# Attention steps that are due within two groups of matmuls, taken ahead of a product's evictions and of weight splits

## The chip, the cores and the metric

The kernel runs on one core of one Trainium2 chip. The metric is device time in microseconds (us), lower is better. Before the change three timed runs gave 1688.29, 1689.68 and 1690.58, a median of 1689.68.

## What is computed

One layer of a decoder trunk in float32, over 2048 tokens of width 1024. `u` is the modulated input; one wide product makes queries, keys, values and gates; a sliding-window attention (16 query heads, 2 key heads, window 128, a learned bias and one "sink" logit per head) and a multi-scale causal pool run side by side; two projections, a gated sum, an output projection and a layer norm follow.

```python
u = x * (1.0 + scale[:, None, :]) + shift[:, None, :]
h = u @ w_in[l]
q, k, v, a_gate, p_in, p_gate, m_a, m_p = jnp.split(h, offsets, axis=-1)
a = sliding_window_sink_attention(q, k, v, sinks[l], bias, mask) * jax.nn.silu(a_gate)
a = a @ w_attn_proj[l]
p = jnp.einsum('bsgc,gcd->bsgd', multiscale_causal_pool(p_in), w_pool_mix[l]).reshape(B, S, POOL_WIDTH)
p = ((p * pool_scale[l]) * jax.nn.silu(p_gate)) @ w_pool_proj[l]
y = jax.nn.sigmoid(m_a) * a + jax.nn.sigmoid(m_p) * p
y = (y @ w_out[l]) * (1.0 + gate[:, None, :])
x = layer_norm(DEEPNORM_ALPHA * x + y, ln_gain[l], ln_bias[l])
```

## The kernel before

**Products.** A float32 operand is split into two halves (`hi`, a rounded copy, and `lo`, the rest), and one matmul becomes three: hi by hi, hi by lo, lo by hi (`mm3`). A "group" is such a trio of 128x128 by 128x512 matmuls, and a "product" is four groups, one after the other, into one PSUM bank (`product`, L295). Two neighbouring output tiles by two halves of the tokens are computed with seven products in place of eight, in Strassen's manner. The class `Quad` holds such a four. Its products are called, in order, B11, T1 (stage F), T2, B21 (stage S), T3, B22 (stage Th) and T4 (stage L). A quad that runs alone keeps T4 for later, when it stands between B11 and T1 of the next quad. The moving operands are the tiles `set_B...` and `set_T...`; in the excerpts below T1, T2, T3 and T4 read set_T_67, set_T_159, set_T_411 and set_T_613, and B11, B21 and B22 read set_B_66, set_B_68 and set_B_459.

**Evictions** (`behind`, L460). After each product comes its follow-up. After B11 ACT copies bank a to a third bank c (`mm<-mm`); after T1 ACT copies bank b to a tile p (`p<-mm`); after T2 DVE writes b = c + p (`mm<-mm,p`), which reads the bank c that T3 accumulates into next, so T3 must wait for it; after T3 DVE writes p = c + p (`p<-mm,p`). Four tiles leave through `consume`, after B21, T3, B22 and T4: one ACT instruction, and for queries and two of the gates one DVE instruction that waits for it (`q_hi` then `q_lo`, or `sig` then `sig`). For the pooled input (`px`) and two other gates ACT alone does it.

**Weight splits** (`split_part`, L431). Weights of a stage are split two or three products ahead: ACT casts them (`CAST w_set<-W`), then DVE (for stage Th of a quad that runs alone, POOL) subtracts to get `lo`. A table made by `plan` says at which product each part stands (`before`); `run` (L488) issues the parts ahead of that product's matmuls.

**Attention steps** (`overlay`, L812). In two phases of the program, one for each half of the tokens, 13 quads run alone, 91 products, and attention is woven in: 64 steps and three more to drain the pipeline. Step n (L922) issues on PE the scores of block n (`lg<-kk,qs`), the transposes of block n-2 (`pt<-ident,L`) and the value matmuls of block n-3 (`pv<-...`). On ACT it issues the scaling of block n-1 (`L<-L` with 192 columns, twice), the cast `pth<-pt`, a copy `o<-pv` and the exponentials of block n (`L<-L` with 193 columns, twice). On DVE it issues a reciprocal, two bias-and-minimum instructions (shown as ISA), the subtraction `ptl<-pt,pth` and two additions `st<-pv,o`. POOL writes a small mark, SP loads the next queries. The scores bank `lg` and the transposes bank `pt` exist once: a step's transposes wait until DVE has done `ptl` of the step ahead.

**When a step comes** (`beat`, L978). `product` calls `beat` after each group. Each call adds `rate` to a credit, and at 1 a step is issued there and then; the first 12 calls of a phase, and some in its middle, are rests. With N = 64 and 364 groups, rate is 67 / 316 = 0.212, so that a step comes every 4.7 groups, at any of the four places of a product. All engines take their instructions in the order in which the program issues them, which the kernel keeps by hand (`Ordered`, L50).

Of the kernel before, what the change touches and what calls it, by code (L numbers as in the profile page):

```python
# [59 lines left out]
def kernel(  # L60
# [81 lines left out]
    def cols(t, n):  # L142
        return t[:, n * CH : (n + 1) * CH]
# [13 lines left out]
    def mm3(acc, whi, wlo, uhi, ulo, start, stop, **kw):  # L157
        mm(acc, whi, uhi, start=start, stop=False, **kw)
        mm(acc, whi, ulo, start=False, stop=False, **kw)
        mm(acc, wlo, uhi, start=False, stop=stop, **kw)  # L160

    def bank(tag="mm"):
        if tag in ("c1", "pv"):
            return phase_ps["now"].tile([P, CH], F32, tag=tag, bufs=phase_ps["pv"] if tag == "pv" else 1, name=tag)
        return ps.tile([P, CH], F32, tag=tag, bufs=4 if tag == "mm" else 1, name=tag)
# [129 lines left out]
    def product(acc, w, name, first=False, i0=0, i1=4, beat=None):  # L295
        t = sets[name]
        hi, lo = w
        for i in range(i0, i1):
            cols = slice(i * P, (i + 1) * P)
            mm3(  # L300
                acc,
                hi[:, cols],
                lo[:, cols],
                t[:, i, 0, :],
                t[:, i, 1, :],
                first and i == 0,
                i == 3,
                skip_group_check=True,
            )
            if beat:  # L310
                beat()
# [3 lines left out]
    def defer(ticks, f, local=False):  # L315
        due.append((now[0] + ticks, len(due), f, local))

    def run_due(every=False, local=False):
        while due and (every or any(d[0] <= now[0] or local and d[3] for d in due)):
            d = min((d for d in due if every or d[0] <= now[0] or local and d[3]), key=lambda d: d[:2])  # L320
            due.remove(d)
            d[2]()

    def at(p, f):
        assert p >= now[0], (p, now[0])
        hooks.setdefault(int(p), []).append(f)
# [5 lines left out]
    def tick():  # L332
        for f in hooks.pop(now[0], ()):
            f()
        now[0] += 1
        run_due()
# [89 lines left out]
    def split_part(ph, q, kind, part):  # L426
        if part == 0 and kind in q.parts:
            q.made = kind
        if kind == getattr(q, "made", None):
            return  # L430
        raw = {"F": q.first, "S": q.second, "Th": q.third, "L": lambda: q.a22}[kind]()  # L431
        if kind == "L":
            if part == 0:
                t = q.parts["L"] = ph.split(*q.rings[kind])
                act.copy(t[:, 0:CH], raw)
            else:
                t = q.parts["L"]
                low(dve, t[:, CH:], raw, t[:, 0:CH])
            return
        if part == 0:  # L440
            hi, lo = q.parts[kind] = [ph.split(x) for x in q.rings[kind]]
            act.copy(by_two(hi), raw)
            return
        hi, lo = q.parts[kind]
        low(pool if kind == "Th" and not q.pair and not q.tail else dve, by_two(lo), raw, by_two(hi))
        if kind == "F":
            q.mid(pool)
            defer(2, lambda q=q: q.keep_sum(1))
        if kind == "S":
            q.late(pool)  # L450

    def weights_of(q, kind, h):
        if kind == "L":
            t = q.parts["L"]
            return t[:, 0:CH], t[:, CH:]
        hi, lo = q.parts[kind]
        return cols(hi, h), cols(lo, h)

    def behind(ph, q, kind, h):
        if kind == "F":  # L460
            if h == 0:
                q.c = bank(("lg", "c1")[q.x] if q.pair else "mm")
                if q.pair and q.x in ph.fresh:
                    t = sets["B11"][:, 0, 0, :]
                    mm(q.c, t[:, 0:P], t, start=True, stop=True, skip_group_check=True)
                    ph.fresh.remove(q.x)
                act.copy(q.c, q.a)
            else:
                q.p5 = ph.p("p5")
                act.copy(q.p5, q.b)  # L470
        elif kind == "S":
            if h == 0:
                if not q.summed:
                    dve.tensor_tensor(q.b, q.c, q.p5, ALU.add)
            else:
                q.consume(ph, 0, 0, q.a)
        elif kind == "Th":
            if h == 0:
                dve.tensor_tensor(q.p5, q.c, q.p5, ALU.add)
                q.consume(ph, 1, 1, q.p5)  # L480
            else:
                q.consume(ph, 0, 1, q.b)
        else:
            q.consume(ph, 1, 0, q.c)
# [3 lines left out]
    def run(phases, products, before, loads):  # L488
        starts = {z["first"]: z for z in phases}
        ph, leave, beat = None, None, None  # L490
        for p, (q, kind, h, name) in enumerate(products):
            if p in starts:
                phase = starts[p]
                if phase["pools"] is not ph:
                    if ph:
                        if leave:
                            leave()
                        run_due(True)
                        ph.__exit__(None, None, None)
                    ph = phase["pools"].__enter__()  # L500
                leave, beat = None, None
                more = phase["enter"](ph, phase)
                if more:
                    beat, leave = more
            assert now[0] == p
            done = q.opened and kind in "FS"
            for z, k, part in before.get(p, ()):
                if not (z.opened and k in "FS"):
                    split_part(ph, z, k, part)
            for z, what in loads.get(p, ()):  # L510
                if what == "w":
                    z.load_w(ph)
                elif what == "last":
                    z.load_last(ph, z.own)
                elif what == "sum":
                    if not z.again:
                        z.sum1()
                        defer(1, lambda z=z: z.keep_sum(0))
                else:
                    z.prefetch(ph, *what)  # L520
            if done:
                if kind == "S" and h:
                    at(p + LATER[q.x, "S"], lambda q=q: behind(ph, q, "S", 1))
                if kind == "F":
                    now[0] += 1
                    continue
            else:
                if kind == "F" and h == 0:
                    q.a, q.b = bank(), bank()
                acc = {"B11": "a", "T1": "b", "T2": "c", "B21": "a", "T3": "c", "B22": "b", "T4": "c"}[name]  # L530
                product(getattr(q, acc), weights_of(q, kind, h), name, kind == "F", beat=beat)
                for f in mids.pop(p, ()):
                    f()
                if q.opened and kind == "L" and q.x:
                    at(p + LATER[q.x, kind], lambda q=q: behind(ph, q, "L", 0))
                elif q.opened and (q.x, kind) in LATER and not h:
                    at(p + 1, lambda q=q: dve.tensor_tensor(q.p5, q.c, q.p5, ALU.add))
                    at(p + LATER[q.x, kind], lambda q=q: q.consume(ph, 1, 1, q.p5))
                else:
                    behind(ph, q, kind, h)  # L540
            tick()
        run_due(True)
        ph.__exit__(None, None, None)
# [247 lines left out]
    def overlay(ph, s, n_slots):  # L791
# [3 lines left out]
        N = KT * U  # L795
# [179 lines left out]
        state = [0, 0.0, 12]  # L975
        rate = (N + 3) / (n_slots - 48.0)

        def beat():  # L978
            n, credit, rest = state
            if rest:  # L980
                state[2] -= 1
                return
            state[1] += rate
            if state[1] >= 1 and n < N + 3:
                step(n)
                state[0] += 1
                state[1] -= 1
                if n == N // 2 - 1:
                    load_k(1)
                    state[2] = 8  # L990
                if n == N // 2 + 2:
                    load_v(1)
                    state[2] = 5
# [689 lines left out]
    for i, (groups, store) in enumerate(parts):  # L1683
        phase(mix_pools, groups, out_part(i, store))
    run(phases, *plan(phases))


# [51 lines left out]
```

## Time and profile before

| | us |
|---|---|
| median of three runs | 1689.68 |
| the profiled execution, its own time | 1685.7 |
| the profiled execution, first to last instruction (span) | 1683.8 |
| first attention phase, the stretch 150 to 470 | 320 |
| second attention phase, the stretch 728 to 1046 | 318 |

The page's first part gives each engine's busy time: PE 98%, DVE 69%, ACT 57%, POOL 35%. PE's granted clock is 90% or more in all of the forty slices of its second part but the second one, and 0.994 in the mean over the span. In a row of the timeline stand the start, the duration, the engine, the instruction with what it writes and reads, and in brackets how long the engine sat idle before and what ended that. Matmuls are pipelined: a row's duration overlaps the next row's start, so the distance between starts is what a matmul costs.

### The profile page before, as it was taken

To read this page: it belongs to the slowest core of one execution; us is meant where nothing else is said; L and a number is where in the kernel's file an instruction comes from. 1 tells how busy PE (TensorE), PEld (TensorE's weight loads), DVE (VectorE), ACT (ScalarE), POOL (GpSimd) and SP (SyncE) were. 2 spreads that over 40 slices of the span, in tenths; PEclk is the share of its full clock that TensorE was granted. 3 is DMA by queue.
4 is the path that set the end of the run, shared out by engine and by line. 5 is a ranking of instruction groups with operands and counts; after the bars stand their busy time and mean duration, and the time that the engine had idled before them with its cause. 6 is when DMAs were issued, how large, how long until landed. Compare 5 with 4: busy or idle time off the path is not lost. (4 is left out here: it accounts for less than half of the span.)

```text
span 1683.8 us, 24835 instructions
## 1 busy us (share of the span) xinstructions
PE 1654.8 (98%) x8146; PEld 1392.7 (83%) x8146; DVE 1164.9 (69%) x2161; ACT 962.7 (57%) x1944; POOL 588.4 (35%) x569
## 2 busy tenths in 40 slices
PE   8999999999999999999999999999999999999997
PEld 8888888888888888888888888888888888888885
DVE  6765666665648779546666666587867785878878
ACT  4555878788743346467877777344544343435453
POOL 3112454645552323323334244222332211114544
PEclk9899999999999999999999999999999999999999
DMA  9499777986557799875566553688968686777443
GB/s 349 137 306 302 197 233 203 265 219 202 173 181 234 267 316 309 274 188 163 172 179 202 151 171 127 222 281 304 347 207 303 230 309 203 264 259 266 151 151 124
DMA packets 340896, 384.77 MB, mean 229 GB/s; under 512 B 152200, under 2 KB 203424, under 8 KB 340640
## 3 DMA queue, kind: packets, MB, share of 16 engines
q1 hardware_dynamic: 334880, 376.99, 69.8%
q10 hardware_dynamic: 5856, 6.18, 1.1%
q8 instruction: 64, 1.05, 0.3%
q14 instruction: 64, 0.52, 0.1%
q0 software_dynamic: 32, 0.02, 0.0%
HBM read 238.91 MB, written 145.78 MB: 228 GB/s over the span
## 5 line engine op out<-in xcount | busy, mean ns | idle before, releaser
L56 PE MATMUL mm<-set_B,w_set 128*128 128x512 f32 x2664 | 651.5, 391 | 0.7 <-DVE w_set L56 0.7
L56 PEld LDWEIGHTS mm<-set_B,w_set 128*128 128x128 f32 x2664 | 496.1, 188 | 103.5 <-DVE w_set L56 1.5
L56 POOL TENSOR_TENSOR W<-W 128x512 f32<-128x512 f32 x185 | 268.0, 1459 | 584.2 <-DVE w_set L56 344.9
L56 PE MATMUL mm<-set_T,w_set 128*128 128x512 f32 x1896 | 463.7, 391 | 1.0 <-POOL w_set L56 0.7
L56 PEld LDWEIGHTS mm<-set_T,w_set 128*128 128x128 f32 x1896 | 349.7, 188 | 73.1 <-POOL w_set L56 1.9
L56 DVE TENSOR_TENSOR w_set<-W,w_set 128x1024 fp32r<-128x1024 f32 x197 | 255.5, 1297 | 107.6 <-ACT w_set L56 93.0
L56 ACT CAST w_set<-W 128x1024 fp32r<-128x1024 f32 x222 | 232.2, 1047 | 95.5 <-PE mm L56 55.6
L56 ACT ACTIVATE L<-L 128x193 f32<-128x193 f32 (+5 forms) x512 | 214.9, 446 | 99.5 <-DVE L L56 98.4
L56 PE MATMUL lg<-set_T,w_set 128*128 128x512 f32 x828 | 201.4, 391 | 1.4 <-DVE w_set L56 1.0
L56 PE MATMUL c<-set_T,w_set 128*128 128x512 f32 x828 | 200.8, 390 | 0.0
L56 PEld LDWEIGHTS lg<-set_T,w_set 128*128 128x128 f32 x828 | 155.1, 188 | 34.9 <-DVE w_set L56 1.8
L56 PEld LDWEIGHTS c<-set_T,w_set 128*128 128x128 f32 x828 | 155.5, 188 | 33.0 <-DVE w_set L56 0.8
L56 DVE TENSOR_TENSOR ptl<-pt,pth 128x512 fp32r<-128x512 f32 (+1 forms) x128 | 86.4, 675 | 117.5 <-ACT pth L56 117.5
L56 POOL TENSOR_TENSOR W<-W,A 128x512 f32<-128x512 f32 x41 | 58.1, 1418 | 271.1 <-DMA A<-in_win_dram 106.6
L56 DVE CUSTOM_DVE_ANT_0 L<-lg,bt,nsink 128x192 f32<-128x192 f32 (+2 forms) x256 | 93.6, 404 | 22.3 <-PE lg L56 21.7
L56 ACT ACTIVATE sig<-mm 128x512 f32<-128x512 f32 x76 | 45.5, 599 | 92.8 <-PE mm L56 89.8
L56 PEld LDWEIGHTS lg<-kk,qs 128*128 128x128 f32 x512 | 76.2, 190 | 15.7 <-issue 4.2
L56 POOL TENSOR_TENSOR w_set<-W,w_set 128x1024 fp32r<-128x1024 f32 x25 | 60.9, 2435 | 77.8 <-ACT w_set L56 69.4
L56 PE MATMUL pt<-ident,L 128*128 128x128 f32 x496 | 76.5, 275 | 5.7 <-DVE ptl L56 5.4
L56 PE MATMUL lg<-kk,qs 128*128 128x192 f32 (+2 forms) x512 | 75.8, 270 | 3.6 <-DMA qs<-q_d 2.9
L56 POOL TENSOR_TENSOR st<-st,ag 128x512 f32<-128x512 f32 x32 | 46.5, 1452 | 84.3 <-DVE st L56 78.5
L56 ACT CAST pth<-pt 128x512 fp32r<-128x512 f32 (+1 forms) x128 | 71.9, 562 | 6.4 <-PE pv L56 5.6
(211 smaller groups left out, 1905.9 us busy)
## 6 DMA issues: line engine op xcount, KB each, us to landing
W<-in_win_dram SPq DMA_DIRECT2D x40, 512.0 KB, 5.8
qs<-q_d SPq DMA_DIRECT2D x128, 128.0 KB, 4.3
sums_d<-W SPq DMA_DIRECT2D x62, 256.0 KB, 3.6
W<-sums_d SPq DMA_DIRECT2D x31, 512.0 KB, 3.6
ain_d<-st SPq DMA_DIRECT2D x56, 256.0 KB, 3.6
A<-in_win_dram SPq DMA_DIRECT2D x42, 256.0 KB, 5.5
q_d<-q_hi SPq DMA_DIRECT2D x32, 256.0 KB, 4.1
q_d<-q_lo SPq DMA_DIRECT2D x32, 256.0 KB, 3.9
```

What stands on the lines that cost most here:

```text
L56: return lambda *args, **kw: self.tc.keep_in_program_order(op(*args, **kw))
```

## The change

`beat` gets an argument. With `early=2.0` it adds nothing to the credit, does nothing during a rest, and issues a step when the credit would reach 1 within two more groups. `run` makes such a call at two places: ahead of the weight splits that stand before a product, and after a product's four groups, ahead of its evictions. Right after a product the credit has not changed by the time of the next product's splits, so there the first call finds what the second one left.

```diff
--- before.py
+++ after.py
@@ -504,6 +504,8 @@
                     beat, leave = more
             assert now[0] == p
             done = q.opened and kind in "FS"
+            if beat and p in before:
+                beat(2.0)
             for z, k, part in before.get(p, ()):
                 if not (z.opened and k in "FS"):
                     split_part(ph, z, k, part)
@@ -529,6 +531,8 @@
                     q.a, q.b = bank(), bank()
                 acc = {"B11": "a", "T1": "b", "T2": "c", "B21": "a", "T3": "c", "B22": "b", "T4": "c"}[name]
                 product(getattr(q, acc), weights_of(q, kind, h), name, kind == "F", beat=beat)
+                if beat:
+                    beat(2.0)
                 for f in mids.pop(p, ()):
                     f()
                 if q.opened and kind == "L" and q.x:
@@ -975,13 +979,16 @@
         state = [0, 0.0, 12]
         rate = (N + 3) / (n_slots - 48.0)
 
-        def beat():
+        def beat(early=0.0):
             n, credit, rest = state
+            if rest and early:
+                return
             if rest:
                 state[2] -= 1
                 return
-            state[1] += rate
-            if state[1] >= 1 and n < N + 3:
+            if not early:
+                state[1] += rate
+            if state[1] + early * rate >= 1 and n < N + 3:
                 step(n)
                 state[0] += 1
                 state[1] -= 1
```

A step that fell behind the first or second group of a product (34 of the 67 in each phase) now stands at the end of the product ahead; one that fell behind the third or fourth group stays. By the credit's arithmetic, 46 of the distances between steps were five groups and 18 were four; now 42 are four, 11 five and 11 seven, beside two longer ones at the pauses in each order.

The first place is the start of the first attention phase, on PE: B21 and T3 of the first quad, and the scores of the first two steps. Set names as above. Before:

```order
L56 MATMUL mm<-set_T_159,w_set 128x512 x12
L56 MATMUL mm<-set_B_68,w_set 128x512 x12
L56 MATMUL mm<-set_T_411,w_set 128x512 x3
L56 MATMUL lg<-kk,qs 128x64 x2
L56 MATMUL lg<-kk,qs 128x128 x2
L56 MATMUL mm<-set_T_411,w_set 128x512 x9
L56 MATMUL mm<-set_B_459,w_set 128x512 x6
L56 MATMUL lg<-kk,qs 128x192 x4
L56 MATMUL mm<-set_B_459,w_set 128x512 x6
```

Now:

```order
L56 MATMUL mm<-set_T_159,w_set 128x512 x12
L56 MATMUL mm<-set_B_68,w_set 128x512 x12
L56 MATMUL lg<-kk,qs 128x64 x2
L56 MATMUL lg<-kk,qs 128x128 x2
L56 MATMUL mm<-set_T_411,w_set 128x512 x12
L56 MATMUL lg<-kk,qs 128x192 x4
L56 MATMUL mm<-set_B_459,w_set 128x512 x12
```

The first step's scores moved from behind T3's first group to the end of B21, and the second step's from the middle of B22 to the end of T3.

The second place is in the second phase, where a gate's quad (`sig`) follows a query's quad (`q_hi`); on ACT, from the copy after B11 to the second step behind it. `pth` marks a step; `q_hi<-mm` is the eviction after T4, `p_...<-mm` the one after T1, and `w_set<-W` the cast for stage Th. Before:

```order
L56 COPY mm<-mm 128x512
L56 ACTIVATE q_hi<-mm 128x512
L56 ACTIVATE L<-L 128x192 x2
L56 CAST pth<-pt 128x512
L56 COPY o_8985<-pv 64x256
L56 ACTIVATE L<-L 128x193 x2
L56 COPY p_9005<-mm 128x512
L56 CAST w_set<-W 128x1024
L56 ACTIVATE L<-L 128x192 x2
L56 CAST pth<-pt 128x512
L56 COPY o_9038<-pv 64x256
```

Now:

```order
L56 COPY mm<-mm 128x512
L56 ACTIVATE L<-L 128x192 x2
L56 CAST pth<-pt 128x512
L56 COPY o_8978<-pv 64x256
L56 ACTIVATE L<-L 128x193 x2
L56 ACTIVATE q_hi<-mm 128x512
L56 ACTIVATE L<-L 128x192 x2
L56 CAST pth<-pt 128x512
L56 COPY o_9026<-pv 64x256
L56 ACTIVATE L<-L 128x193 x2
L56 COPY p_9041<-mm 128x512
L56 CAST w_set<-W 128x1024
```

The first of the two steps moved ahead of T4's eviction, the second ahead of T1's eviction and the cast. A little later in the same quad, DVE around the eviction after T2, `mm<-mm,p`. Before:

```order
L56 TENSOR_TENSOR ptl<-pt,pth 128x512
L56 TENSOR_TENSOR st<-pv,o_9038 64x128 x2
L56 TENSOR_TENSOR mm<-mm,p_9005 128x512
L56 RECIPROCAL L<-L 128x2
L56 ISA L<-lg,bt,nsink 128x192
L56 ISA L 128x1
L56 ISA L<-lg,bt,nsink 128x192
L56 ISA L 128x1
L56 TENSOR_TENSOR ptl<-pt,pth 128x512
```

Now:

```order
L56 TENSOR_TENSOR st<-pv,o_9026 64x128 x2
L56 RECIPROCAL L<-L 128x2
L56 ISA L<-lg,bt,nsink 128x192
L56 ISA L 128x1
L56 ISA L<-lg,bt,nsink 128x192
L56 ISA L 128x1
L56 TENSOR_TENSOR ptl<-pt,pth 128x512
L56 TENSOR_TENSOR st<-pv,o_9083 64x128 x2
L56 TENSOR_TENSOR mm<-mm,p_9041 128x512
```

A whole step, with its subtraction `ptl`, moved ahead of the addition after T2.

The third place is two quads earlier, a quad of pooled input, on DVE: splits of stage F and L (`w_set`) and a step. Before:

```order
L56 TENSOR_TENSOR st<-pv,o_8414 64x128 x2
L56 TENSOR_TENSOR w_set<-W,w_set 128x1024
L56 TENSOR_TENSOR w_set<-A_7825,w_set 128x512
L56 RECIPROCAL L<-L 128x2
L56 ISA L<-lg,bt,nsink 128x192
L56 ISA L 128x1
L56 ISA L<-lg,bt,nsink 128x192
L56 ISA L 128x1
L56 TENSOR_TENSOR ptl<-pt,pth 128x512
```

Now:

```order
L56 RECIPROCAL L<-L 128x2
L56 ISA L<-lg,bt,nsink 128x192
L56 ISA L 128x1
L56 ISA L<-lg,bt,nsink 128x192
L56 ISA L 128x1
L56 TENSOR_TENSOR ptl<-pt,pth 128x512
L56 TENSOR_TENSOR st<-pv,o_8454 64x128 x2
L56 TENSOR_TENSOR w_set<-W,w_set 128x1024
L56 TENSOR_TENSOR w_set<-A_7860,w_set 128x512
L56 TENSOR_TENSOR p_8363<-mm,p_8363 128x512
```

The two splits moved from ahead of a step to behind it, and stand right ahead of the addition after T3.

## The prediction

> **What bounds the kernel.** I read the page first, then the stretches of the two attention phases, since the change touches nothing outside them, then PE's waits there.
>
> ```profile
> span 1683.8 us, 24835 instructions
> PE 1654.8 (98%) x8146; PEld 1392.7 (83%) x8146; DVE 1164.9 (69%) x2161; ACT 962.7 (57%) x1944; POOL 588.4 (35%) x569
> ...
> 150.00:470.00 320.00, 314.44 (x1733) 269.07 (x1732) 198.56 (x599) 250.54 (x644) 161.14 (x182) 1.00 0.76 217
> ...
> 728.00:1046.00 318.00, 313.98 (x1755) 270.76 (x1754) 203.15 (x597) 244.31 (x629) 109.78 (x126) 1.00 0.60 169
> ```
>
> PE is busy 98% of the span, and in both phases all but 5.6 and 4.0 us. ACT is busy 250.54 of 320 us (78%) and 244.31 of 318 (77%), DVE 62 and 64%. So PE is the bound, and the order of ACT's and DVE's work matters only where PE waits for it:
>
> ```profile
> PE pt L56 <- DVE ptl L56: 3.4, 9, 0.7
> PE lg L56 <- DMA qs<-q_d: 1.3, 1, 1.3
> ...
> PE pt L56 <- DVE ptl L56: 2.0, 5, 0.7
> PE lg L56 <- DMA qs<-q_d: 1.6, 1, 1.6
> ```
>
> The first two rows are the first phase, the others the second. The transposes wait for the subtraction `ptl` of the step ahead, 3.4 + 2.0 us in 14 places, and the first scores of a phase for a DMA. That is all the change can win: 5.4 us as idle time, perhaps 9 with the slower starts around it. It removes and adds no instruction; it only moves steps.
>
> **How a step hangs together.** A stretch of the second phase on PE, where a gate's quad follows a query's (steps 25 to 29):
>
> ```profile
> 847.12 3.58 PE L56 MATMUL mm<-set_B,w_set 128*128 128x512 f32 x15
> 850.54 0.59 PE L56 MATMUL lg<-kk,qs 128*128 128x192 f32 x4
> 850.96 0.61 PE L56 MATMUL pt<-ident,L 128*128 128x128 f32 x4
> ...
> 855.32 0.59 PE L56 MATMUL lg<-kk,qs 128*128 128x192 f32 x4
> 856.00 0.65 PE L56 MATMUL pt<-ident,L 128*128 128x128 f32 x4
> ...
> 856.97 2.92 PE L56 MATMUL mm<-set_T,w_set 128*128 128x512 f32 x12
> 859.73 0.59 PE L56 MATMUL lg<-kk,qs 128*128 128x192 f32 x4
> 860.56 0.66 PE L56 MATMUL pt<-ident,L 128*128 128x128 f32 x4 [0.25 <-DVE ptl L56]
> ...
> 867.73 2.24 PE L56 MATMUL mm<-set_T,w_set 128*128 128x512 f32 x9
> ```
>
> Fifteen matmuls take 850.54 - 847.12 = 3.42 us, so 0.23 each, 0.69 a group, 2.75 a product. Undisturbed transposes start 0.42 after the scores (850.96 - 850.54), and a step takes about 1.4 us of PE (0.42, and 0.97 from its transposes to the next matmuls, 856.00 to 856.97). Two steps four groups apart start 4.1 us apart, five groups 4.8.
>
> ```profile
> 843.18 0.16 DVE L56 RECIPROCAL L<-L 128x2 f32<-128x2 f32 x1
> 843.43 0.81 ACT L56 ACTIVATE L<-L 128x192 f32<-128x192 f32 x2 [2.12 <-DVE L L56]
> 844.14 0.56 ACT L56 CAST pth<-pt 128x512 fp32r<-128x512 f32 x1
> 844.74 0.69 DVE L56 TENSOR_TENSOR ptl<-pt,pth 128x512 fp32r<-128x512 f32 x1 [0.74 <-ACT pth L56]
> 845.35 0.57 DVE L56 TENSOR_TENSOR st<-pv,o 64x128 f32<-64x128 f32 x2
> 845.80 0.19 ACT L56 ACTIVATION_READ_ACCUMULATOR L<-L 128x1 f32 x1
> 846.67 0.63 ACT L56 ACTIVATE q_hi<-p 128x512 fp32r<-128x512 f32 x1 [0.68 <-DVE p L56]
> 847.34 0.69 DVE L56 SCALAR_TENSOR_TENSOR q_lo<-p,q_hi 128x512 fp32r<-128x512 f32 x1 [0.70 <-ACT q_hi L56]
> ```
>
> This is one step's chain: reciprocal to scaling 0.25, to `pth` 0.71, to `ptl` 0.60, to its end 0.69; `st` ends 2.74 after the reciprocal, the exponentials 1.85 after `pth`. It zigzags between ACT and DVE, and an eviction ahead of it adds its own zigzag (0.63 + 0.69): in the second row ACT sat idle 2.12 us until DVE came to the step. The next step's reciprocal waits for the exponentials of this one. So the chain is nearly serial, and a step moved ahead of evictions gets a short chain, while what it passed gets a long one.
>
> **The change, place by place.**
>
> *Starts of the phases.*
>
> ```profile
> 156.88 0.86 PE L56 MATMUL mm<-set_T,w_set 128*128 128x512 f32 x3
> 159.07 0.63 PE L56 MATMUL lg<-kk,qs 128*128 128x64 f32 x4 [1.34 <-DMA qs<-q_d]
> ...
> 732.13 0.66 PE L56 MATMUL lg<-kk,qs 128*128 128x192 f32 x4 [1.61 <-DMA qs<-q_d]
> ```
>
> The first scores wait for their queries, which are issued at the phase's start, as before. Now they stand ahead of the three matmuls (in both phases) that covered 0.69 us of that wait. **+0.7 twice, +1.4.** Nothing hides this.
>
> *The stretch above: a step behind B11, T4, T1 and T2 each, and T4 of the quad ahead leaves through ACT and DVE* (steps 26 to 29, and 47 to 50 in the same pattern; two places in each phase).
>
> ```profile
> 855.26 0.69 DVE L56 TENSOR_TENSOR ptl<-pt,pth 128x512 fp32r<-128x512 f32 x1 [0.73 <-ACT pth L56]
> 856.53 0.57 ACT L56 COPY mm<-mm 128x512 f32<-128x512 f32 x1
> 861.09 0.59 ACT L56 COPY p<-mm 128x512 f32<-128x512 f32 x1
> 861.58 1.05 ACT L56 CAST w_set<-W 128x1024 fp32r<-128x1024 f32 x1
> 862.52 0.81 ACT L56 ACTIVATE L<-L 128x192 f32<-128x192 f32 x2
> 864.93 0.68 DVE L56 TENSOR_TENSOR mm<-mm,p 128x512 f32<-128x512 f32 x1
> ```
>
> Step 26 does not move; its `ptl` ends at 855.95, so step 27's transposes start at 856.00, as before, but the group that PE did ahead of them is now behind: 0.69 lost. Step 27's chain no longer has T4's eviction ahead: copy at 856.53, scaling 857.1, `pth` 857.8, `ptl` done 859.1, exponentials 859.65. So step 28, at 859.73, starts its transposes at 860.15 and not at 860.56: 0.41 won, 0.28 behind. Then T4's eviction (0.63 + 0.69 with its hand-over) puts step 28's reciprocal at 861.0; scaling 861.25, `pth` 861.95, exponentials done 863.8. Now the copy to p and the cast come (861.09 to 862.52 in the rows, 1.43): step 29's scaling 865.25, `pth` 865.95, `ptl` 866.55, `st` done 867.75, and only then the addition `mm<-mm,p`, done 868.45. PE: step 28 ends 861.1, T2 863.9, step 29 865.25, B21 868.0. T3 writes the bank that this addition reads, so it starts at 868.5; before, with the same steps done, it started at 867.73 (the last PE row), for the addition had gone at 864.93. **+0.75 four times, +3.0.**
>
> The other T2 ends that got a step (seven a phase) have one at B21's end too, so T3 comes 1.4 later (5.5 us after T2's end) and a chain of 2.74 + 0.69 with a cast ahead (1.43) fits. I cost them nothing; if that slack is gone each costs up to 0.75.
>
> *The last two gates' quads* (steps 53 to 55 and 59 to 61).
>
> ```profile
> 1017.38 0.69 PE L56 MATMUL lg<-kk,qs 128*128 128x192 f32 x4
> 1018.81 0.66 PE L56 MATMUL pt<-ident,L 128*128 128x128 f32 x4 [0.74 <-DVE ptl L56]
> ```
>
> Step 60 already waits (1.43 after its scores, not 0.42) and moves one group ahead: 0.69 lost in each phase, as the `ptl` it waits for does not move. At step 54 most of the group is covered; about 0.25 lost. **+1.8 in all.**
>
> *Splits that now follow a step in a pooled quad* (the third place of the change).
>
> ```profile
> 841.45 1.21 DVE L56 TENSOR_TENSOR w_set<-W,w_set 128x1024 fp32r<-128x1024 f32 x1
> 842.58 0.68 DVE L56 TENSOR_TENSOR w_set<-A,w_set 128x512 fp32r<-128x512 f32 x1
> ...
> 813.78 1.72 DVE L56 TENSOR_TENSOR w_set<-A,w_set 128x512 fp32r<-128x512 f32 x1 [0.24 <-ACT w_set L56]
> ```
>
> DVE used to do them while it waited for step 18; now step 18 is awaited first, and 1.9 us of splits (1.21 + 0.68) stand ahead of steps 19 and 20 and so of step 21's transposes. Between nothing (a slack of about one group swallows it) and +1.0 in each phase: I take half, **+1.0 in all**. The same form of split took 0.68 and 1.72 us; the longer one ran beside POOL work. "GPSIMD Engine Reference" of the Trainium skill, section 1, says that GpSimd's SBUF interfaces are shared with VectorE, with contention for DVE instructions that have two SBUF inputs; the two rows agree. By that rule the splits, now beside POOL's five gate operations, cost their long form, and the sum would take the upper end, 1.0 more.
>
> *Won.*
>
> ```profile
> 772.62 0.66 PE L56 MATMUL pt<-ident,L 128*128 128x128 f32 x4 [0.38 <-DVE ptl L56]
> ```
>
> Step 9 waits behind a pile of evictions, with PE idle 0.38. Step 7, moved to T3's end, lets that pile be done earlier: at best **-0.35 twice, -0.7**. Evictions and splits otherwise have two or three products of slack (5 to 8 us) and take the delay of one chain.
>
> **The sum:** 1.4 + 3.0 + 1.8 + 1.0 - 0.7 = +6.5 us. The profiled execution took 1685.7 (span 1683.8), so it would become 1692.2; the three timed runs lie higher, with a median of 1689.68, and against that I predict **1696.2**.
>
> **Rivals.**
> - *Faster.* Moved steps have the short chain, so all waits for `ptl` vanish (5.4 us idle) and T3 never waits: -5.4 + 1.4 = -4.0, 1685.7. For it: the waits named are exactly of this kind, and ACT idles ahead of scalings. It decides if the steps behind B11, which don't move, end `ptl` within 4.5 us of their scores; the stretch above shows 855.95 - 850.54 = 5.4. Chance 0.12.
> - *An exchange.* Waits are won and lost alike, and only the starts and a little remain: +1 to +3, about 1692. For it: delays in a chain that PE leads are partly made up later. Chance 0.26.
> - *Much slower.* T3 waits at all T2 ends with a step, 14 more by 0.5: +7 on the sum, 1703. The weights of T3 may be late as well, since their cast now waits behind a step. Chance 0.15.
> - *It doesn't do what it says.* The call ahead of the splits indeed never issues a step that the call behind a product didn't; but the order of instructions shows half the steps moved, so this rival is out.
>
> My forecast, a loss of 4 to 10 us, has 0.47. About 0.2% (3.4 us) is what a measurement of this kernel can tell from no change. Slower by more than that: 0.47 + 0.15 = 0.62; within: 0.26; faster: 0.12. The range reaches from the faster rival, 1686, to the much slower one, 1704.
>
> **What would show it.** Right: PE's wait for the queries grows from 1.3 and 1.6 to 2.0 and 2.3; waits of PE for `ptl` stay at 5 us or more, at the steps behind T4; a new wait of PE for DVE's `mm<-mm,p`, some 2 us in four places. Wrong: no such new wait, or the waits for `ptl` gone; or T3 waiting for POOL's `w_set`.

## The result and the profile after

The changed kernel took 1695.69 us (median of six runs, 1693.9 to 1697.66) beside 1689.71 for the kernel before (six runs, 1686.37 to 1690.58). The ratio is 1.0038, with a 95% interval of 1.0025 to 1.0051: 6.4 us slower, between 4.2 and 8.6. The profiled execution took 1693.9 us. Two single executions of the kernels reported below ran at a mean granted clock of 0.565 and 0.555 (2718 us in `not_t4`, 2763 us in the kernel before) and are left out of all medians and ratios.

The page of the kernel after, its first part (busy time, share of the span, instructions), then PE's waits in the first attention phase (150 to 475 us) and in the second (728 to 1055 us): total idle us, times, longest.

```profile
span 1692.0 us, 24814 instructions
PE 1655.8 (98%) x8146; PEld 1391.7 (82%) x8146; DVE 1168.5 (69%) x2161; ACT 961.2 (57%) x1944; POOL 592.2 (35%) x569
...
PE pt L56 <- DVE ptl L56: 4.7, 9, 0.8
PE lg L56 <- DMA qs<-q_d: 1.8, 1, 1.8
PE mm L56 <- DVE mm L56: 1.4, 2, 0.7
PE lg L56 <- DVE L L56: 0.9, 3, 0.4
...
PE pt L56 <- DVE ptl L56: 3.2, 6, 0.7
PE lg L56 <- DMA qs<-q_d: 1.4, 1, 1.4
PE lg L56 <- DVE L L56: 0.7, 2, 0.5
PE mm L56 <- DVE mm L56: 0.4, 2, 0.2
```

The work is the same: 8146 matmuls, and PE busy for 1655.8 us against 1654.8. What grew is idle time inside the phases. The waits for `ptl` went from 3.4 + 2.0 to 4.7 + 3.2 us, and a row that did not exist stands at 1.4 + 0.4: PE waits for DVE's `mm<-mm,p`, the addition that T3 has to wait for, in four places. The scores' waits for DVE grew to 0.9 + 0.7; in the kernel before there was this row in the first phase and none in the second:

```profile
PE lg L56 <- DVE L L56: 0.7, 2, 0.5
```

One of those places, in the second phase: PE and DVE of the kernel after, steps 27 to 29 and T3.

```profile
859.40 0.59 PE L56 MATMUL lg<-kk,qs 128*128 128x192 f32 x4
860.50 0.66 PE L56 MATMUL pt<-ident,L 128*128 128x128 f32 x4 [0.51 <-DVE ptl L56]
...
864.22 0.59 PE L56 MATMUL lg<-kk,qs 128*128 128x192 f32 x4
864.65 0.60 PE L56 MATMUL pt<-ident,L 128*128 128x128 f32 x4
...
868.34 0.59 PE L56 MATMUL lg<-kk,qs 128*128 128x192 f32 x4
868.76 0.60 PE L56 MATMUL pt<-ident,L 128*128 128x128 f32 x4
869.67 2.94 PE L56 MATMUL mm<-set_B,w_set 128*128 128x512 f32 x12
872.83 2.32 PE L56 MATMUL mm<-set_T,w_set 128*128 128x512 f32 x9 [0.22 <-DVE mm L56]
...
870.90 0.69 DVE L56 TENSOR_TENSOR ptl<-pt,pth 128x512 fp32r<-128x512 f32 x1 [1.17 <-ACT pth L56]
871.51 0.57 DVE L56 TENSOR_TENSOR st<-pv,o 64x128 f32<-64x128 f32 x2
872.00 0.68 DVE L56 TENSOR_TENSOR mm<-mm,p 128x512 f32<-128x512 f32 x1
```

Step 27 now waits for `ptl` (1.10 from scores to transposes instead of 0.68); step 28 no longer does (0.43 instead of 0.83); and the addition, which DVE did at 864.93 before, ahead of step 29's chain, comes behind `ptl` and `st` of that step, so that T3 starts 3.16 after B21 did, where twelve undisturbed matmuls take 2.75. The pattern is the one forecast. It holds at this place, at steps 48 to 50 of the same phase and at steps 27 to 29 of the first phase; at steps 48 to 50 of the first phase PE waits at step 48 instead (0.22 at its scores and 0.76 at its transposes), and T3 does not wait.

The largest loss was not forecast. Behind the pause in the middle of the second phase, at steps 34 to 36, POOL, ACT and PE of the kernel after:

```profile
900.76 2.33 POOL L56 TENSOR_TENSOR st<-st,ag 128x512 f32<-128x512 f32 x1 [7.92 <-DVE st L56]
903.18 4.24 POOL L56 TENSOR_TENSOR st<-st 128x512 f32<-128x512 f32 x3
907.36 1.31 POOL L56 TENSOR_TENSOR W<-W 128x512 f32<-128x512 f32 x1
...
908.70 1.05 ACT L56 CAST w_set<-W 128x1024 fp32r<-128x1024 f32 x1 [3.12 <-POOL W L56]
911.18 0.80 ACT L56 ACTIVATE L<-L 128x192 f32<-128x192 f32 x2 [1.43 <-DVE L L56]
...
906.37 0.59 PE L56 MATMUL lg<-kk,qs 128*128 128x192 f32 x4
...
911.80 0.69 PE L56 MATMUL lg<-kk,qs 128*128 128x192 f32 x4 [0.49 <-DVE L L56]
913.23 0.66 PE L56 MATMUL pt<-ident,L 128*128 128x128 f32 x4 [0.74 <-DVE ptl L56]
```

The same place in the kernel before:

```profile
893.66 1.28 POOL L56 TENSOR_TENSOR W<-W 128x512 f32<-128x512 f32 x1 [6.38 <-ACT px L56]
894.88 0.66 POOL L56 COPY L<-nsink 128x2 f32<-128x2 f32 x1
898.22 1.30 POOL L56 TENSOR_TENSOR st<-st,ag 128x512 f32<-128x512 f32 x1 [2.69 <-DMA vv<-v_d]
899.60 4.89 POOL L56 TENSOR_TENSOR st<-st 128x512 f32<-128x512 f32 x3
...
900.24 1.04 ACT L56 CAST w_set<-W 128x1024 fp32r<-128x1024 f32 x1
```

A step that completes a block of attention output gives POOL the gate work of that block (`st<-st,ag` and three `st<-st`), to be issued at the next call of the queue of postponed work. Steps 33 and 34 come earlier now, and so POOL's gate work of 6.6 us (900.76 to 907.36) is issued ahead of the `W<-W` that makes weights. ACT's cast waits 3.12 us for that `W<-W`; the scaling of step 35 stands behind the cast on ACT and behind the next split on DVE; and step 36 waits twice, 0.49 at its scores and 0.74 at its transposes. Before, `W<-W` had gone first, at 893.66. From the scores of step 32 to those of step 40, neither of which moves, the second phase took 924.44 - 884.14 = 40.30 us before and takes 931.28 - 889.30 = 41.98 now; with the first phase, where step 36 waits in the same way, this place costs 3.2 us.

### The profile page after: what moved, and what is told of

The parts are those of the page before. It is cut to its first block, busy times and chain, and to the rows that moved or that the text cites. A ratio compares the mean times of both kernels' runs of the same rounds, so it can differ in the third digit from the quotient of the medians.

```text
span 1692.0 us, 24814 instructions
## 1 busy us (share of the span) xinstructions
PE 1655.8 (98%) x8146; PEld 1391.7 (82%) x8146; DVE 1168.5 (69%) x2161; ACT 961.2 (57%) x1944; POOL 592.2 (35%) x569
## 4 chain that ended last, share of the span: by engine, by line
PE 73%; ACT 7%; DVE 6%; issue 5%; DMA 5%; POOL 2%; SPq 1%; ACTq 0%; DVEq 0%; POOLq 0%
PE mm L56 45%; PE lg L56 12%; PE c L56 10%; PE pv L56 4%; PE pt L56 3%; ACT L L56 3%; DVE w_set L56 2%; ACT w_set L56 1%; ACT pth L56 1%; POOL st L56 1%; DVE wide L56 1%; DMA W<-in_wap_dram 1%; DVE ptl L56 1%; SPq L56 1%; POOL W L56 1%
```

## The experiments

Each kernel is the changed one with one edit, timed beside the kernel before on the same chip. The rounds ran on different chips, so kernels are compared by their ratios to the kernel before. In the table, "idle for DVE" is the sum of PE's waits for `ptl`, `L` and `mm` in both phases, from the same view as the rows above (before: 3.4 + 0.7 + 2.0 = 6.1), and the last column is the ratio less one, times 1689 us. The median of the kernel before was 1689.71 for the first four, 1687.18 for `only_start`, `only_rest` and `wins_five`, 1689.05 for `picked` and 1689.01 for the other four.

| kernel | steps taken early | idle for DVE, us | median, us | ratio (95%) | against before, us |
|---|---|---|---|---|---|
| the change | all 34, of which 32 have scores | 11.3 | 1695.69 | 1.0038 (1.0025 to 1.0051) | +6.4 |
| add_first | all; addition ahead of step | 13.7 | 1702.31 | 1.0077 (1.0062 to 1.0092) | +13.0 |
| gate_late | all; gate work one tick later | 8.7 | 1694.37 | 1.0028 (1.0016 to 1.0040) | +4.7 |
| not_t4 (three runs) | all but those at T4's end | 13.1 | 1699.14 | 1.0069 (1.0047 to 1.0092) | +11.7 |
| splits_only | only ahead of splits | 14.1 | 1703.54 | 1.0082 (1.0066 to 1.0098) | +13.8 |
| only_start | 0, 1 | 5.4 | 1689.68 | 1.0014 (1.0001 to 1.0026) | +2.4 |
| only_wins | 5 to 7, 11, 12, 16 to 18 | 4.6 | 1685.29 | 0.9986 (0.9976 to 0.9996) | -2.4 |
| only_rest | 22 to 24, 37 to 39, 43 to 45 | 7.2 | 1689.54 | 1.0008 (0.9997 to 1.0019) | +1.4 |
| only_mid | 27 to 29, 48 to 50 | 7.6 | 1689.61 | 1.0006 (0.9996 to 1.0017) | +1.0 |
| only_gate | 33, 34 | 8.5 | 1691.54 | 1.0021 (1.0012 to 1.0030) | +3.5 |
| only_last | 54 to 56, 60, 61 | 6.0 | 1688.68 | 1.0003 (0.9993 to 1.0012) | +0.5 |
| wins_five | 5 to 7, 11, 12 | 5.5 | 1686.55 | 0.9995 (0.9983 to 1.0007) | -0.8 |
| picked | the gains of both phases | 5.2 | 1686.60 | 0.9992 (0.9983 to 1.0002) | -1.4 |

**First round: one mechanism at a time, all else as in the change.**

`add_first` issues T2's addition ahead of the step that is taken early there:

```diff
+                ahead = beat and name == "T2"
+                if ahead:
+                    behind(ph, q, kind, h)
                 if beat:
                     beat(2.0)
...
-                else:
+                elif not ahead:
                     behind(ph, q, kind, h)
```

> Changed kernel, but after T2 the addition mm<-mm,p is issued ahead of the early step; where the step stands on PE stays. Theory (T3 waits for an addition that stands behind a whole step on DVE): PE's waits for DVE's mm<-mm,p, idle 1.4 + 0.4 us in the changed kernel, go to 0, and T3 starts without delay in the stretch with steps 26 to 29; time 1 to 3 us below the changed kernel, about 1693. Rival (the delay is only shown there; the chain of steps is late anyway and would stop PE at the next transposes): the waits for ptl, 4.7 + 3.2 us, grow by as much as the others fall, and the time stays at 1695.7.

The wait of PE for `mm<-mm,p` is gone, as the theory wanted, and yet the kernel is 7 us slower than the change instead of faster; the rival's waits for `ptl` grew by more than the others fell. Its waits in the first phase:

```profile
PE pt L56 <- DVE ptl L56: 5.9, 11, 0.8
PE lg L56 <- DVE L L56: 2.4, 4, 1.4
```

The wait moved to other steps and grew. The addition waits for ACT's copy to p, and DVE with it, so that the step's reciprocal comes only behind it (at 875.51 here, in the second phase):

```profile
874.78 0.70 DVE L56 TENSOR_TENSOR mm<-mm,p 128x512 f32<-128x512 f32 x1 [0.72 <-ACT p L56]
```

Put ahead of the step, the addition thus delays that step's chain. How the delay reaches the later waits was not followed step by step. The largest is at step 60 of the first phase, with the granted clock behind it (windows: PE, PEld, DVE, ACT, POOL busy; then PE's clock, the DMA share, GB/s):

```profile
451.95 0.69 PE L56 MATMUL lg<-kk,qs 128*128 128x192 f32 x4 [1.42 <-DVE L L56]
453.38 0.66 PE L56 MATMUL pt<-ident,L 128*128 128x128 f32 x4 [0.74 <-DVE ptl L56]
454.40 4.45 PE L56 MATMUL mm<-set_T,w_set 128*128 128x512 f32 x12
...
454.00:456.00 2.00, 2.00 (x9) 1.71 (x8) 1.04 (x6) 1.98 (x6) 0.13 (x1) 0.56 0.47 146
456.00:458.00 2.00, 2.00 (x7) 1.54 (x7) 1.26 (x4) 1.55 (x6) 0.00 (x0) 0.58 0.68 195
458.00:460.00 2.00, 2.00 (x16) 1.86 (x15) 1.06 (x6) 0.81 (x2) 0.00 (x0) 1.00 0.53 192
```

Two waits that follow each other, 1.42 and 0.74, and then the clock stands at 0.56 and 0.58 for about 4 us: twelve matmuls take 4.45 us where they take 2.9 elsewhere. So here the waits cost some 1.5 us more than themselves; at the same step of the second phase, with waits of 1.00 and 0.74, the clock stayed at 1.00. Putting the addition first thus does not remove the loss: it is handed on, and most of what is added, 3.0 us in the profiles, lies between steps 51 and 62.

`gate_late` keeps all steps, and postpones POOL's gate work of an early step by one more call of the queue:

```diff
-                    defer(1, lambda: finish(jj, tt), True)
+                    defer(wait[0], lambda: finish(jj, tt), True)
...
-        state = [0, 0.0, 12]
+        state, wait = [0, 0.0, 12], [1]
...
+            wait[0] = 2 if early else 1
```

> Changed kernel, but a step that is taken early leaves its attention gate work (st<-st,ag and its three or none st<-st on POOL) to the tick at which it came before, so that the weight sum W<-W stands ahead of it on POOL again. Theory (POOL's gate operations ahead of W<-W hold up the cast for stage S, and with it step 35): in both phases the wait at step 36, lg 0.5 and transposes 0.7 us idle, vanishes; time 2 to 3 us below the changed kernel. Rival (step 36 waits because step 35 comes after a pause of nine groups and meets all evictions at once): it stays.

At the place shown above POOL now takes `W<-W` first, and no step waits there:

```profile
900.15 1.79 POOL L56 TENSOR_TENSOR W<-W 128x512 f32<-128x512 f32 x1 [9.24 <-ACT w_set L56]
901.90 1.29 POOL L56 TENSOR_TENSOR st<-st,ag 128x512 f32<-128x512 f32 x1
903.28 4.78 POOL L56 TENSOR_TENSOR st<-st 128x512 f32<-128x512 f32 x3
```

The idle time fell by 2.6 us, as wanted, and from step 32 to step 40 both phases take what they took before the change, within 0.02 us, where the change added 3.2. The cost by the ratio fell by 1.7 only (from 6.4 to 4.7); the ten runs spread from 1690.64 to 1698.07, so the two numbers do not contradict each other, but the time alone does not settle it.

`not_t4` takes no step early at T4's end:

```diff
-            if beat and p in before:
+            if beat and p in before and products[p - 1][3] != "T4":
...
-                if beat:
+                if beat and name != "T4":
```

> Changed kernel, but no step is taken early at the end of T4, so that steps 27, 48, 54 and 60 stand behind T1's first or second group as before, five groups behind their predecessor. Theory (the step behind T4 meets transposes bank pt still unread; each costs up to the 0.69 us of a group): the waits for ptl at these steps fall by up to 0.69 each, the sum of PE's waits for ptl from 7.9 to some 5.5 us idle, but those at steps 28 and 49 (0.4 each, gone in the changed kernel) come back; time 0 to 2 us below the changed kernel. Rival (a wait of a step is only moved, by one group of matmuls, and the time is set by ACT's and DVE's work): no change of the sum, 1695.7.

A miss: 5 us slower than the change by the ratio, though with three runs the intervals overlap (7.9 to 15.5 against 4.2 to 8.6); in the profile the waits grew from 11.3 to 13.1. Step 27 stays behind T4's eviction and no longer waits in the second phase (0.2 in the first), but step 28, taken early, now starts 3.6 us behind it (4.8 in the change), while step 27's chain still stands behind the evictions of B11 and T4. It waits for step 27's `ptl` with the full 1.43 from scores to transposes; in the second phase:

```profile
865.94 0.69 PE L56 MATMUL lg<-kk,qs 128*128 128x192 f32 x4
867.37 0.66 PE L56 MATMUL pt<-ident,L 128*128 128x128 f32 x4 [0.74 <-DVE ptl L56]
```

So the distance to the step ahead counts, not only the order at one place: here, moving step 28 and not step 27 is worse than moving both.

`splits_only` leaves out the call behind a product, so that a step is taken early only ahead of splits, behind the evictions:

```diff
                 product(getattr(q, acc), weights_of(q, kind, h), name, kind == "F", beat=beat)
-                if beat:
-                    beat(2.0)
```

> Changed kernel with the call behind a product taken out: a step is early only ahead of a product's weight splits, behind the evictions; where a product has no splits ahead of it no step is early. Theory: the addition after T2 is ahead of the step, so no wait of T3 for mm<-mm,p; steps behind the evictions of T4 have the longer chain, so the waits for ptl at the steps after them stay at about those of the kernel before (5.4 us idle); time between the two kernels, about 1692. Rival (putting steps ahead of splits is what costs, not ahead of evictions): as slow as the changed kernel, 1695 to 1696.

The slowest of all. Steps 1, 7, 27, 48 and 60 have no splits at their place and stay where they were, so that 28, 49 and 61 come as close behind them as in `not_t4` and wait as they do there; the others stand as early on PE as in the change, but behind the evictions on ACT and DVE. PE's waits for `ptl` rise to 8.1 and 5.3 us, from the 4.7 and 3.2 of the change. Of the two calls, it is the one ahead of the evictions that keeps the loss small. Step 36 does not wait in this kernel: steps 33 and 34 are as early on PE, but issued behind the call of the queue, and POOL takes `W<-W` (at 909.21) ahead of the gate work (at 910.79).

**Second round: the change cut into six sets of steps, which together are all of it but the drain steps 65 and 66.** The edit, with another tuple in each:

```diff
-            if rest and early:
+            if early and (rest or n not in (27, 28, 29, 48, 49, 50)):
                 return
```

> Of all moved steps only 27, 28, 29 and 48, 49, 50 of each phase are taken early; all others stay where they were before. Theory (the term of the stretch stands by itself): T3 waits for DVE's mm<-mm,p in three or four places by 0.5 to 1.0 us, the transposes of steps 27 and 48 lose what those of 28 and 49 win, together +2.5 to +3.0 us of PE's waits over before, time 1692.2 to 1692.7. Rival (exchange): the waits come back at other steps and the time is within 1 us of before, 1689 to 1690.5.

> Only steps 33 and 34 of each phase are taken early. Theory (POOL's five gate operations of step 34 go ahead of its W<-W, on which ACT's cast to w_set waits, and with it step 35): PE waits 1.4 to 1.6 us at step 36 of each phase as in the changed kernel, nowhere else more than before, +3.0 us, time 1692.7. Rival (that wait needs other moved steps as well, 37 or those of the quad ahead): no wait at step 36 and the time of before, 1689.7.

> Only steps 5, 6, 7, 11, 12, 16, 17 and 18 of each phase are taken early, at whose places the changed kernel waits less. Theory (the gains are independent of the losses): the waits at steps 9, 11 and 14 vanish, step 21 changes by 0.3 at most, -1.5 to -2 us of waits, time about 1688. Rival (the gain is passed on as waits of later steps): the same waits in sum as before, 1689.7.

> Only steps 54, 55, 56, 60 and 61 of each phase are taken early. Theory of the prediction: +1.8 us, one group lost at step 60 of each phase (0.69) and a little at 54, time 1691.5. Rival (read from the changed kernel's trace): step 60 wins as much as it loses, step 54 loses 0.7 and T3 behind step 56 waits 0.95 in the first phase, +1.0 us in all, time 1690.7.

> Only steps 0 and 1 of each phase are taken early. The prediction's term: the wait for the queries grows by 0.7 in each phase, to 2.2 and 2.5, +1.4 us, time 1690.4 to 1691.1. Rival (that wait is set by when the queries land, which differs by more than 0.7 from run to run: 1.2 to 2.9 us in the profiles so far without the early start): the wait lies anywhere in 1.2 to 2.9, the time is that of before within 1 us, and where a wait is longer than 2 us the granted clock may be near 0.55 for the next 3 to 4 us, which adds 1 to 2 us to that profile.

> Only steps 22, 23, 24, 37, 38, 39, 43, 44 and 45 of each phase are taken early. Theory (what is left of the changed kernel's loss is here and at the starts): the waits at steps 41 and 42 of the first phase grow by 0.7 and 0.5 and at 42 of the second by 0.2, +1.4 us, step 31 may win 0.3; time 1690.1 to 1691. Rival (41 and 42 wait because of steps 33 and 34 ahead): no change of waits, time of before.

The six together give +2.4 - 2.4 + 1.4 + 1.0 + 3.5 + 0.5 = +6.4 us, which is what the whole change measures. Each has an interval of some 1.5 to 2 us to either side, so this agreement is in part luck. The profiles say more, by the time between the scores of two steps that do not move, one ahead of a place and one behind it: that time hardly differs between profiles in which nothing moves there (mostly by less than 0.1 us, in a few cases by 0.3, and once by 0.8, where PE waits for a DMA of values). Summed over steps 4 to 62 of both phases, the sets without `only_start` add 6.2 us by themselves, and the change adds 6.1. So no large part is missing, and the parts hardly need each other.

`only_gate` has the loss at step 36 by itself, in both phases:

```profile
906.00 1.29 POOL L56 TENSOR_TENSOR W<-W 128x512 f32<-128x512 f32 x1
...
907.33 1.05 ACT L56 CAST w_set<-W 128x1024 fp32r<-128x1024 f32 x1 [3.12 <-POOL W L56]
...
910.43 0.69 PE L56 MATMUL lg<-kk,qs 128*128 128x192 f32 x4 [0.49 <-DVE L L56]
911.85 0.66 PE L56 MATMUL pt<-ident,L 128*128 128x128 f32 x4 [0.73 <-DVE ptl L56]
```

The same 3.12 on ACT and the same two waits on PE as in the change, and +3.5 us (2.0 to 5.1) of time. With `gate_late`, where both steps move and POOL's order is kept and the waits vanish, the cause of these waits is shown.

`only_wins` is faster than before. Its waits in the two phases:

```profile
PE pt L56 <- DVE ptl L56: 2.3, 6, 0.7
...
PE pt L56 <- DVE ptl L56: 1.8, 5, 0.7
```

Step 9 starts its transposes 0.45 after its scores (before 0.98, with the 0.38 of idle time that the prediction shows):

```profile
772.21 0.59 PE L56 MATMUL lg<-kk,qs 128*128 128x192 f32 x4
772.66 0.66 PE L56 MATMUL pt<-ident,L 128*128 128x128 f32 x4
```

`only_mid` has the T3 waits (0.7 us idle in one place of the first phase, 0.5 in two of the second) and 1.5 more idle time for DVE, but costs +1.0 us (-0.7 to +2.9) and not 2.5 to 3.0; the interval reaches to both theories. `only_last` (+0.5, -1.2 to +2.0) lies nearer to the reading of the trace, but its interval takes in the prediction's 1.8 as well. `only_rest` has the waits at steps 41 and 42 of the first phase in part, and others at 27 and 48 there, while 27 and 48 of the second phase win 0.25 each: +1.4 (-0.5 to +3.2).

`only_start` waits 2.6 and 1.9 us for the queries, above the 2.2 expected of it in the first phase and below the 2.5 in the second. Over all profiles the six kernels with steps 0 and 1 early wait 2.0 and 1.8 us in the mean (1.5 to 2.6 and 1.4 to 2.2), the eight others 1.7 and 1.3 (1.0 to 2.8 and 1.0 to 1.6). The early start is thus worth about 0.8 of wait in both phases together, less than the 1.4 of the prediction, but the spread from run to run is larger than the difference, and 1.4 is not excluded.

**Third round: what is worth keeping.**

> Only steps 5, 6, 7, 11 and 12 of each phase are taken early (the set that won, without 16, 17 and 18). Theory: the waits at 9, 11 and 14 vanish as there, the wait of step 21 in the second phase (0.34, put down to splits that now follow step 18) is absent, and step 21 of the first phase keeps its 0.37 of before: -1.9 to -2.2 us of waits, time 1686 to 1687.5. Rival (step 21's wait comes from elsewhere): 0.34 remains at step 21 of the second phase. If the gain of the first such kernel was chance, the time is that of before.

Here step 21 of the second phase waits no longer, and step 21 of the first keeps its wait, so the splits pushed behind step 18 are what cost 0.34 there. The gain in time is smaller than that of the eight steps, -0.8 (-2.9 to +1.2), which does not tell it from nothing. In the profiles the place itself wins 1.8 to 2.2 us, between steps 4 and 15 of both phases, in each of the seven kernels that move all of steps 5, 6, 7, 11 and 12, the change among them.

`picked` uses another tuple in each phase:

```diff
-            if rest and early:
+            if early and (rest or n not in picked[s]):
                 return
...
+        picked = (5, 6, 7, 11, 12, 16, 17, 18, 27, 28, 60, 61), (5, 6, 7, 11, 12, 22, 23, 24, 43, 44, 45)
```

> Taken early are steps 5, 6, 7, 11, 12, 16, 17, 18, 27, 28, 60 and 61 of the first phase and 5, 6, 7, 11, 12, 22, 23, 24, 43, 44 and 45 of the second, picked from the waits of the runs so far. Theory (each wait is set by the steps just ahead of it and by nothing else): in the first phase 9, 11, 14, 21 and 42 win 1.4 us, 27 to 31 win 0.6 with no wait of T3 (step 29 isn't moved), 60 wins 0.5; in the second 9 and 11 win 1.0, 27 and 48 win 0.25 each, so -4.0 us, ratio 0.9976, time 1683.5 to 1685.5. Rival (waits are passed on when places are combined): the gain is that of the eight steps alone, about -2 us, ratio 0.9988; if T3 still waits behind step 29 of the first phase by 0.97, the term of the stretch doesn't hang on step 29.

With step 29 left where it was, T3 waits nowhere, so at the one place where this was tried (steps 27 to 29 of the first phase) its wait does hang on the step behind T2. Nothing is won there either, though: step 28 no longer waits, and steps 27 and 31 wait as much more. In the second phase all gains came as expected: four waits are left, 1.6 us. In the first they did not: step 42 waits as before, and step 60 waits 1.2 at its scores instead of winning; in `only_last`, where steps 54 to 56 move too, it does not wait there. The ratio, 0.9992, cannot be told from 1. The best kernel is `only_wins`, a gain of 2.4 us with an interval from 0.7 to 4.1; the two kernels like it point the same way, but each of their intervals takes in no change.

## Why the prediction came out right, and where it was wrong

The forecast was +6.5 us; the change costs 6.0 in the medians, 6.4 by the ratio. As a sum it was right. Set by set its terms are less good than the sum. The last column is read from the profile of the change alone, by the time between steps that do not move (4 to 15, 15 to 26, 26 to 32 with 46 to 51, 32 to 40, 40 to 46, 51 to 62; for the starts, the waits for the queries):

| term | forecast, us | measured with these steps alone, us | in the change's profile, us |
|---|---|---|---|
| starts of the phases | +1.4 | +2.4 (0.2 to 4.4) | +0.2 |
| the stretch, steps 27 to 29 and 48 to 50 | +3.0 | +1.0 (-0.7 to +2.9) | +2.6 |
| last two gates' quads | +1.8 | +0.5 (-1.2 to +2.0) | +0.9 |
| splits behind step 18, and step 9 won | +1.0 - 0.7 | -2.4 (-4.1 to -0.7) | +0.2 - 2.2 |
| steps 33 and 34 | nothing | +3.5 (2.0 to 5.1) | +3.2 |
| all others | nothing | +1.4 (-0.5 to +3.2) | +1.4 |

- **Starts.** The mechanism is as described; in the mean of the profiles the wait grew by 0.8 and not 1.4. The term was no bound either: behind a longer wait the clock can fall, as the last section shows, and that the prediction did not have.
- **The stretch.** In three of the four places the mechanism is right to the instruction: step 27 loses, step 28 wins, T3 waits for the addition. The four waits are not quite in the four places named (in the first phase the second is behind step 56, not 50), and they are 1.8 us of idle time in the profile. The term was taken a little high, 3.0 against 2.6 in the profile: in the second phase T3 lost 0.4 (3.16 less 2.75) beside a loss at step 27 and a gain at 28 of 0.4 each, where 0.75 in all had been worked out; in the first phase the two places lost 0.8 and 0.9. The time of these steps alone (+1.0) cannot tell the forecast from nothing.
- **Last gates' quads.** Steps 60 were to lose 0.69 each. In the profile of the change, step 60 of the first phase no longer waits at its scores (0.48 before) and still waits 0.74 at its transposes, and `picked` against `only_last` says that this needs steps 54 to 56 ahead; the second phase gains a wait of 0.23 there. The loss of the first phase is at step 54 (0.59) and at T3 behind step 56 (0.67). The size was wrong for lack of the steps ahead in the calculation.
- **Splits in a pooled quad.** Over-sized: +1.0 forecast; by the starts of step 21's scores and transposes, 0.34 lost in the second phase and 0.19 won in the first. The page "GPSIMD Engine Reference" of the Trainium skill, section 1, was weighed for it. The contention it tells of is here: at step 18 of the second phase `st<-st,ag` beside the splits took 2.33 us, against 1.29 before, and the smaller split 1.63, against the 0.68 that the prediction shows elsewhere. But before the change that split had run beside POOL's `W<-W` and taken 1.72, so it did not become longer, and the upper end of the term did not come. (POOL's gate work there is four operations, not five.)
- **Won.** Step 9 won what was said. Steps 11 and 14 won as well, and were not seen: T3's wait at 11 and the scores' wait at 14 vanished.
- **The step of the sum that failed** is the half-sentence that evictions and splits "otherwise have two or three products of slack" and take the delay of one chain. It looked at DVE and ACT. POOL's queue was not followed: a moved step issues POOL's gate work as well, and at steps 33 and 34 that work passed the `W<-W` that the next cast waits for. By itself it costs 3.5 us (2.0 to 5.1), and 3.2 in the profile, more than any other term there. The steps counted as nothing cost 1.4 more. Losses set too high and a gain set too low came to about as much, and so the sum was near the mark by luck.

Of the rivals, "faster" fell (PE's waits for `ptl` grew instead of vanishing), and so did "T3 waits at all T2 ends": there are four such waits, not eighteen. "An exchange" is not told apart from the forecast by the times of `only_mid`, `only_last` and `only_rest`, but it does not hold for the change: its interval of 4.2 to 8.6 lies above +3. What was to show it right is there (new waits of PE for the addition in four places, waits for `ptl` of 5 us and more); the wait for the queries was 1.8 and 1.4 in that profile and not 2.0 and 2.3, which one profile cannot show.

## What to carry to other kernels

Where two chains of small instructions zigzag between two engines, moving one ahead of the other often only moved the wait to the next instruction that needed the other; look for the places where a wait exists, and move only there. When a piece of work is moved, follow it on every queue that it issues to, the idle ones too: the dearest loss here came through an engine that was busy 35% of the time. And cutting a change into sets by position, each timed alone, found a gain of 2.4 us (0.7 to 4.1) inside a loss of 6.4. Where the times of such sets are too noisy, the distance in the profile between two pieces of work that do not move is a sharper measure.

## What the runs showed of the hardware

In this kernel a wait of PE of about 2 us can be followed by half the clock. Of the 28 phase starts profiled, nineteen waits for the queries of 1.0 to 1.8 us were followed by matmuls at full clock; of nine waits of 1.9 to 2.8 us, seven were followed by some 3.4 us (6.8 behind the longest) in which a 128x512 matmul came every 0.43 us instead of every 0.23. The kernel `only_start`, behind its wait of 2.6 us:

```profile
159.00:161.00 2.00, 2.00 (x7) 1.60 (x6) 0.89 (x4) 1.72 (x6) 0.00 (x0) 0.59 1.06 371
161.00:163.00 2.00, 2.00 (x8) 1.55 (x7) 1.74 (x3) 0.16 (x1) 0.80 (x1) 0.56 1.23 268
163.00:165.00 2.00, 2.00 (x12) 1.70 (x11) 1.37 (x5) 1.56 (x7) 2.00 (x2) 1.00 1.16 273
```

Eight matmuls that each lose 0.2 us (six to eight did, thirteen behind the longest wait) are 1.6 us, nearly as much as the wait itself; that it makes a part of the spread from run to run is likely but was not tried by itself. "TensorE: Matmul & The Clock Gate" of the Trainium skill, part 1, states a spacing of 426.7 ns for a gated clock, and the runs agree with 0.43; it puts the gate behind an idle window of about 3.4 us, and here 1.9 to 2.8 us, or two waits of 1.42 and 0.74 with four small matmuls between them, were enough in eight of ten cases.
